# Mixer steps written as two streams between the dense matmuls of a hybrid decoder block

## The chip, the cores and the metric

One core of a Trainium2 chip runs the whole kernel. TensorE (PE) multiplies, VectorE (DVE) and ScalarE (ACT) do elementwise work, GpSimd (POOL) a little, and SyncE (SP) and ACT issue the DMAs. The metric is the device time of one execution in microseconds (us). The kernel before takes 2914.36 us, the median of 3 runs (2911.06 to 2918.03).

## The reference, cut to what matters

One layer over 2048 positions of width 1024, in float32:

```python
h = rmsnorm(x, norm1_g) * (1 + sc1) + sh1
p = h @ w_in                                  # 27 column blocks of 128
ya = rglru_mixer(...)                         # gated linear recurrence, 2 blocks of 128 columns
yb = hgrn2_mixer(...)                         # 6 heads of 64, chunks of 64 positions
yc = rwkv7_mixer(...)                         # 6 heads of 64, delta rule: S = S*w - (S k) (k a)' + v k'
y = concatenate([ya, yb, yc]) * mix_beta
x = x + g1 * (y @ w_out)
h = rmsnorm(x, norm2_g) * (1 + sc2) + sh2
x = x + g2 * ((silu(h @ w_gate) * (h @ w_up)) @ w_down)   # inner width 2816
return rmsnorm(x, final_g)
```

The rows of `p` of one time block must be there before a mixer of that block starts, and all mixers of a block before its product with `w_out`. The state of each mixer goes from one time block to the next.

## The kernel before, in words

The 2048 positions are four time blocks of 512. Activations stand with the 128 columns of a column block on the partitions and 512 positions along the free axis, so a dense product is a row of 128x512 matmuls. Each factor is split into a rounded high part and a low part (`wh`, `wl`; `hh`, `hl`), and each product is three matmuls, `hh*wh`, `hl*wh`, `hh*wl`, written in `project` (line 247). There are 9696 of these **dense matmuls**: 2592 for `w_in`, and 1776 in each block for `w_out`, gate, up and down. ACT rounds a weight tile (`wh`), DVE takes the rest (`wl`, line 220). Four blocks of `w_in` are done first, their results stored in DRAM (`pd`), then `w_out` and the feed-forward part block by block, with the mixers' results (`yd`) read back by `load_y`.

At the end of `w_out` of each block stands the **norm boundary**: the last column's residual (`stt`, DVE), its square, the sum over columns on PE (`rstd_of`, lines 295 to 298), the root (ACT), the scaled input of the feed-forward part (`make_h`, DVE and ACT), and only then the next dense matmul.

The **mixers** are small fp32 matmuls between elementwise steps. For a block, `mixers(b)` writes: the low-rank part `lora`; `rwkv` for head pairs 0 and 1 together; `hgrn` 0; `rglru` 0; `rwkv` for pair 2; `hgrn` 1; `rglru` 1; `hgrn` 2. In `rwkv`, `rwkv_chunks` prepares the chunk operands: after a sum over heads (`blocksum`, lines 256 and 257) come some ten DVE operations of 128x512 and then the matmuls of line 564. Next the small triangular matrices are stored to DRAM (`nd`), and `invert` loads them into `big` by DMAs on ACT's queue (lines 612 and 613; 4 for two pairs, 8 for one), eliminates on DVE, stores the result (`xd`), loads it into `GIQ` and joins halves on PE (lines 643 and 651). Then eight chunks follow each other, each in three steps of PE with DVE and ACT between them (lines 679/681, 692, 697/699). `rglru` loads its rows, convolves on DVE and multiplies (lines 867 and 871). Tiles of `rwkv` have the tag `tr` (9 buffers) and the PSUM tag `pm`, those of the other two `th` (8 buffers) and `ph` (one bank).

The order on each engine is made by the framework's scheduler: it walks through the program by its own estimate of when operands and buffers are ready, and gives each engine, of the instructions that are ready, the one with the lowest priority number. `level(name)` sets these numbers: "out" first, then "load" (weights), "feed" (inputs and norms), "mix", and "dense" last. Within a level the number follows the order of writing. So before, a mixer's matmul goes ahead of any dense matmul as soon as the scheduler holds it for ready, and on DVE and ACT `rwkv` has the right of way over the `hgrn` and `rglru` that are written after it. Once built, each engine runs its list strictly in this order: a matmul that is not ready holds all behind it.

Of the kernel before, what the change touches and what calls it, by code (L numbers as in the profile page):

```python
# [49 lines left out]

@with_exitstack
def hybrid_kernel(ctx, tc, x, par, ada_w, w_in, rgw, igw, w_up, a_up, g_up, w_out,
                  w_gate, w_upf, w_down, cst, msk, out):
    nc = tc.nc
    V, A, G, PE, SP = nc.vector, nc.scalar, nc.gpsimd, nc.tensor, nc.sync
# [193 lines left out]

    def blocksum(src, p, tag):  # L250
        n = src.shape[1]
        hi = tile_of(tag, R)[:, 0:n]
        lo = tile_of(tag, R)[:, 0:n]
        p = p[:, 0:n]
# [217 lines left out]
    def low_rank(i, cols, l1):  # L472
        pz = pm_()
        PE.matmul(pz, LW[i][:, cols], l1, start=True, stop=False)
        PE.matmul(pz, LW[2 + i][:, cols], l1, start=False, stop=True)
        return pz

    def lora(b):

        t = shifted(b, 9, tr_())  # L480
# [36 lines left out]
    def rwkv_chunks(b, u, pr, ld, nd):  # L517

        k = shifted(b, 3 + pr, tr_())
# [12 lines left out]
        rn = rsqrt_of(sq, blocksum(sq, pm_(), "tr"), 1.0, eps_k)  # L532
# [27 lines left out]
        for q in range(0, NCH, 2):  # L560
            ps = pm_()
# [8 lines left out]
        for q in range(0, NCH, 4):  # L570
            p = pm_()
            for c in range(q, q + 4):
                PE.transpose(p[:, (c - q) * 128:(c - q + 1) * 128], BK[:, c, :], ident)
# [8 lines left out]
    def rwkv_values(b, u, pr, r, VS):  # L582

        v = shifted(b, 6 + pr, tr_())
        pb, _ = blocksum(r, pm_(), "tr")
        p = pm_()
        for g in range(NG):
            PE.transpose(p[:, g * 128:(g + 1) * 128], v[:, g * 128:(g + 1) * 128], ident)
# [12 lines left out]
    def invert(b, prs, nd):  # L601
# [8 lines left out]
        for g in range(ng):  # L610
            part = slice(nb * g, nb * g + nb)
            A.dma_start(NL[part], nd)
            A.dma_start(NX[part, 0:32 // ng], n4[:, :, g, :])
        for j in range(1, 31):
# [17 lines left out]
        X1, TT = tr_(), tr_()  # L632
        n = nu * NCH * 32
        xv, tv = (a[:, 0:n].rearrange("p (u c t) -> p u c t", u=nu, t=32) for a in (X1, TT))
        half = [(slice(64 * e, 64 * e + 32), slice(64 * e + 32, 64 * e + 64)) for e in range(2)]
        p = pm_()
        pv = p.rearrange("p (u c t) -> p u c t", u=2, t=32)
        for e, (lo, up) in enumerate(half):
            for u in range(nu):
                V.transpose(X1[lo, u * 256:u * 256 + 256], GIQ[lo, :, u, 0, e, 0:32])  # L640
            for u in range(nu):
                for c in range(NCH):
                    PE.matmul(pv[up, u, c], GIQ[lo, c, u, 0, e, 32:64], xv[lo, u, c], start=True, stop=True)
        for e, (lo, up) in enumerate(half):
            V.tensor_copy(TT[up, 0:n], p[up, 0:n])
        p = pm_()
        pv = p.rearrange("p (u c t) -> p u c t", u=2, t=32)
        for e, (lo, up) in enumerate(half):
            for u in range(nu):
                for c in range(NCH):  # L650
                    PE.matmul(pv[lo, u, c], tv[up, u, c], GIQ[up, c, u, 0, e, 32:64], start=True, stop=True)
# [4 lines left out]
    def rwkv(b, prs, ld):  # L656
# [3 lines left out]
        ops = [rwkv_chunks(b, u, pr, ld, nd) for u, pr in enumerate(prs)]  # L660
        invert(b, prs, nd)
        VS = big_().rearrange("p (c u e v) -> p c u e v", u=2, e=2, v=64)
        bonus = [rwkv_values(b, u, pr, op[3], VS) for u, (pr, op) in enumerate(zip(prs, ops))]
# [9 lines left out]
        for q in range(0, NCH, cq):  # L673
            py = pm_().rearrange("p (c u e t) -> p c u e t", c=cq, u=nu, t=64)
            for c in range(q, q + cq):
                pcn = pp.tile([128, 2, 3, 64], F, name="pc", bufs=1)
                both = [VS[:, c, u].rearrange("p e v -> p (e v)") for u in range(nu)]
                for u, (KG, BK, we, r) in enumerate(ops):
                    PE.matmul(pcn[:, u, 0:2, :], KG[:, c, 0].rearrange("p e t -> p (e t)"), both[u], start=True, stop=True)  # L679
                for u, (KG, BK, we, r) in enumerate(ops):  # L680
                    PE.matmul(py[:, c - q, u], both[u], KG[:, c, 1], start=(c == q and u == 0), stop=False,
# [5 lines left out]
                for u, (KG, BK, we, r) in enumerate(ops):  # L687
                    for e in range(2):
                        s, o = HD[e]
                        act(hw[s, u], VS[s, c, u, e, :], AF.Copy, scale=we[s, c:c + 1])  # L690
                for u in range(nu):
                    PE.matmul(pcn[:, u, 2, :], GIQ[:, c, u, 0].rearrange("p e t -> p (e t)"), rs[:, u], start=True,
                              stop=True)
                V.tensor_copy(VS[0:64, c, 0:nu, 0, :], pcn[0:64, 0:nu, 2, :])
                act(VS[64:128, c, 0:nu, 1, :], pcn[64:128, 0:nu, 2, :])
                for u, (KG, BK, we, r) in enumerate(ops):
                    i1 = PE.matmul(pcn[:, u, 0:2, :], BK[:, c, :], both[u], start=True, stop=True)  # L697
                for u in range(nu):
                    order(PE.matmul(py[:, c - q, u], both[u], GIQ[:, c, u, 1], start=False, stop=True,
# [10 lines left out]
        for y, bn, pr in zip(ys, bonus, prs):  # L710
# [3 lines left out]
            rn = rsqrt_of(sq, blocksum(sq, pm_(), "tr"), 1.0 / 64, eps_g)  # L714
# [4 lines left out]
            A.dma_start(l2, ld[3, 0, :, 0:TB])  # L719
            pg = pm_()  # L720
            PE.matmul(pg, gup[:, cols], l2, start=True, stop=True)
# [10 lines left out]
    def hgrn(b, pr):  # L732
        p = load_p(th_(), 7 + pr, b)
# [12 lines left out]
        pb, _ = blocksum(qk, ph_(), "th")  # L746
# [3 lines left out]
        VS, AQ = big_().rearrange("p (two e c v) -> two p e c v", two=2, e=2, v=64)  # L750
        p = ph_()
        for g in range(NG):
            PE.transpose(p[:, g * 128:(g + 1) * 128], v[:, g * 128:(g + 1) * 128], ident)
# [7 lines left out]
        for l in range(6):  # L761
# [6 lines left out]
            if l == 0:  # L768

                V.tensor_mul(pair, qv[:, :, 1, 0], kv[:, :, 0, 0])  # L770
                pb, _ = blocksum(pair, ph_(), "th")
# [3 lines left out]
            elif l < 4:  # L775

                for e in range(2):
                    s, o = HD[e]
                    z = QZ[s, :, e, :].rearrange("p c (n w) -> p c n w", w=w)
                    act(z, qv[s, :, 1, :].rearrange("p (c n) w -> p c n w", c=NCH))  # L780
                p = ph_()
                for c in range(NCH):
                    PE.matmul(p[0:64, c * 64:c * 64 + 64], k[:, c * 64:c * 64 + 64], QZ[:, c].rearrange("p e t -> p (e t)"),
# [9 lines left out]
            else:  # L793
                p = (ph_(),) * 2
                for c in range(NCH):
                    for j in range(0, 64, 2 * w):
                        for e in range(2):
                            s, o = HD[e]
                            PE.matmul(p[e][o.start + j:o.start + j + w, c * w:c * w + w],
# [15 lines left out]
        KT = c64(th_())  # L815
        p = ph_()
        for g in range(NG):
            PE.transpose(p[:, g * 128:(g + 1) * 128], k[:, g * 128:(g + 1) * 128], ident)
# [5 lines left out]
        for e in range(2):  # L824
            s, o = HD[e]
            p = ph_()
            for c in range(NCH):
                PE.matmul(p[s, c * 64:c * 64 + 64], KT[o, c, :], VS[o, e, c, :], start=True, stop=True)  # L828
            V.tensor_copy(VS[s, e, 0, :], Sc[s, pr, :])
            for c in range(NCH):  # L830
                dst = VS[s, e, c + 1, :] if c + 1 < NCH else Sc[s, pr, :]
                stt(dst, VS[s, e, c, :], dv[s, c:c + 1], p[s, c * 64:c * 64 + 64], OP.mult, OP.add)
        po = ph_()
        for e in range(2):
            s, o = HD[e]
            for c in range(NCH):
                PE.matmul(po[s, c * 64:c * 64 + 64], VS[:, e, c, :], AQ[:, e, c, :], start=True, stop=True)  # L837
# [3 lines left out]
        rn = rsqrt_of(sq, blocksum(sq, ph_(), "th"), 1.0 / 64, eps_n)  # L841
        V.tensor_mul(od, od, rn)
        p = load_p(th_(), 13 + pr, b)
# [12 lines left out]
    def rglru(b, j):  # L856
        up = tile_of("th")
# [6 lines left out]
        for i in range(1, 4):  # L864
            stt(u, up[:, i:i + TB], pc("conv_w", 2 * i + j), u, OP.mult, OP.add)
        p = ph_()
        PE.matmul(p, rgt[:, j, :], u, start=True, stop=True)
        r = th_()
        act(r, p, AF.Sigmoid, bias=pc("rg_b", j))
        p = ph_()  # L870
        PE.matmul(p, igt[:, j, :], u, start=True, stop=True)
# [26 lines left out]
        rn = rsqrt_of(sq, blocksum(sq, ph_(), "th"), 1.0 / 64, eps_n)  # L898
# [4 lines left out]
    def w_in_products(h, cols, side):  # L903

        n = 0
        while n < len(cols):
# [3 lines left out]
            for i, b in enumerate(h):  # L910
                for j, (c, p) in enumerate(zip(cs_, project(h[b], *ws))):
                    with level("feed"):
# [5 lines left out]
                        SP.dma_start(pd[c, :, b * TB:(b + 1) * TB], t)  # L918
                    next(side, None)
            n += len(cs_)  # L920

    def mixers(b):
        with level("mix"):
            lr = lora(b)
            rwkv(b, (0, 1), lr)
            hgrn(b, 0)
            rglru(b, 0)
            rwkv(b, (2,), lr)
            hgrn(b, 1)
            rglru(b, 1)  # L930
            hgrn(b, 2)

    def load_y(b):
        ys = []
# [83 lines left out]
    mixers(0)  # L1018
# [64 lines left out]
```

## Time and profile before

| | |
|---|---|
| median of 3 runs | 2914.36 us |
| the profiled execution | 2919.62 us |
| its span, first to last instruction | 2917.8 us |
| PE busy, weight loads busy | 2767.1 us (95%), 2213.5 us (76%) |
| DVE busy, ACT busy | 1945.5 us (67%), 1480.5 us (51%) |
| mean granted TensorE clock | 0.975 of 2.4 GHz |

Matmuls overlap in the record: a dense one is listed with 399 ns while the next starts 227 ns later. Idle time of PE is what is left of the span: 150.7 us. In the waits view a row tells who waited for whom, the total time, how often, and the longest. The windows view gives for a stretch its length, then for PE, weight loads, DVE, ACT and POOL the busy time and the count of instructions, then the granted clock, the share of DMA and GB/s.

### The profile page before, as it was taken

The page shows a single profiled execution, that of the slowest core. Times are in us where ns is not written, and L with a number is a line of the kernel's source. Part 1 is how long each engine was busy: PE and PEld are TensorE (multiplying, and loading weights), DVE is VectorE, ACT ScalarE, POOL GpSimd, SP SyncE. Part 2 cuts the span into 40 slices and gives each one's busy share as a digit, 9 for nine tenths or more (in the row PEclk, how much of TensorE's full clock was granted, in tenths as well). Part 3 has the DMA queues.
Part 4 walks back from the last instruction along what each step waited for, and adds up shares of the span by engine and source line. Part 5 has one row for each costly group of instructions (what it writes and reads, how often), then busy time and mean ns, then how long its engine had stood idle before and what let it go on. Part 6 is the DMA issues. An engine that isn't in the chain of part 4 may idle for free. (4 is left out here: it accounts for less than half of the span.)

```text
span 2917.8 us, 41296 instructions
## 1 busy us (share of the span) xinstructions
PE 2767.1 (95%) x14842; PEld 2213.5 (76%) x14842; DVE 1945.5 (67%) x4112; ACT 1480.5 (51%) x2472; POOL 86.1 (3%) x67
## 2 busy tenths in 40 slices
PE   7999999999998999999989999998799999999998
PEld 6777777777776777887767778776577888788886
DVE  7676577676757877777787687768776444744345
ACT  5434753564375467536754765377456423533233
POOL 2000000000001000000100000010000001000000
PEclk9999998999998999999989999999899999999999
DMA  7643455454235234341442434233423333433332
GB/s 252 190 138 102 137 182 172 131 159 130 80 124 168 76 103 127 114 107 57 139 145 74 140 111 121 80 113 111 131 77 102 98 98 114 150 98 96 96 98 87
DMA packets 242589, 352.27 MB, mean 121 GB/s; under 512 B 72912, under 2 KB 78544, under 8 KB 242384
## 3 DMA queue, kind: packets, MB, share of 16 engines
q1 hardware_dynamic: 160144, 285.55, 31.6%
q10 hardware_dynamic: 82240, 64.09, 8.3%
q8 instruction: 117, 1.92, 0.3%
q14 instruction: 88, 0.72, 0.1%
HBM read 293.92 MB, written 55.62 MB: 120 GB/s over the span
## 5 line engine op out<-in xcount | busy, mean ns | idle before, releaser
L247 PE MATMUL pd<-hh,wh 128*128 128x512 f32 x3232 | 1288.4, 399 | 33.5 <-ACT hh L78 27.1
L247 PE MATMUL pd<-hl,wh 128*128 128x512 f32 x3232 | 1289.7, 399 | 2.7 <-DVE hl L81 1.4
L247 PE MATMUL pd<-hh,wl 128*128 128x512 f32 x3232 | 1288.2, 399 | 1.1 <-DVE wl L220 1.0
L78 ACT ACTIVATE wh<-wr 128x512 fp32r<-128x512 f32 (+1 forms) x752 | 463.6, 620 | 885.0 <-PE pd L247 707.9
L247 PEld LDWEIGHTS pd<-hh,wh 128*128 128x128 f32 x3232 | 615.1, 191 | 170.0 <-ACT hh L78 32.4
L220 DVE TENSOR_TENSOR wl<-wr,wh 128x512 fp32r<-128x512 f32 (+1 forms) x752 | 511.6, 684 | 321.3 <-ACT wh L78 314.3
L247 PEld LDWEIGHTS pd<-hl,wh 128*128 128x128 f32 x3232 | 614.9, 190 | 137.2 <-DVE hl L81 6.3
L247 PEld LDWEIGHTS pd<-hh,wl 128*128 128x128 f32 x3232 | 615.3, 190 | 131.5 <-issue 5.1
L81 DVE SCALAR_TENSOR_TENSOR xs<-pd,Q,xs 128x512 f32<-128x512 f32 x224 | 167.4, 748 | 152.2 <-PE pd L247 130.4
L78 ACT ACT_TABLE_LOAD x174 | 223.2, 1283 | 3.8 <-PEq L1074 0.7
L78 ACT ACTIVATE th<-th 128x512 f32<-128x512 f32 (+2 forms) x153 | 93.4, 611 | 56.3 <-DVE th L81 14.0
L967 DVE TENSOR_TENSOR xs<-pd,xs 128x512 f32<-128x512 f32 x88 | 60.7, 689 | 83.0 <-PE pd L247 82.7
L78 ACT ACTIVATE xs<-pd 128x512 f32<-128x512 f32 x140 | 82.5, 589 | 45.0 <-PE pd L247 41.5
L78 ACT ACTIVATE hh<-xs 128x512 fp32r<-128x512 f32 x120 | 74.1, 628 | 43.0 <-DVE xs L967 29.1
L78 ACT ACTIVATE hw<-big,we 64x64 f32<-64x64 f32 x192 | 66.2, 345 | 52.1 <-DVE big L81 45.9
L78 ACT ACTIVATE xs<-xs 128x512 f32<-128x512 f32 x77 | 47.8, 627 | 67.9 <-DVE xs L81 38.5
L78 ACT ACTIVATE tr<-tr 128x512 fp32r<-128x512 f32 (+4 forms) x112 | 69.5, 627 | 10.6 <-DVE tr L81 4.7
L539 POOL MEMSET KG<- 64x1024 f32 x24 | 22.7, 946 | 1701.0 <-PE pc L679 839.0
L216 POOL TENSOR_TENSOR hl<-xs,hh 128x512 fp32r<-128x512 f32 x32 | 49.0, 1555 | 642.6 <-ACT hh L78 601.0
L220 DVE TENSOR_TENSOR hl<-xs,hh 128x512 fp32r<-128x512 f32 x88 | 60.7, 690 | 5.6 <-ACT hh L78 1.3
L81 DVE SCALAR_TENSOR_TENSOR big<-pc,we,hw 64x64 f32<-64x64 f32 x168 | 47.6, 283 | 24.7 <-PE pc L697 21.6
L564 PE MATMUL pm<-KG,BK 128*128 128x256 f32 x192 | 50.5, 409 | 11.7 <-DVE KG L553 8.1
(229 smaller groups left out, 2638.7 us busy)
## 6 DMA issues: line engine op xcount, KB each, us to landing
wr<-in_w_gate SPq DMA_DIRECT2D x176, 256.0 KB, 2.6
wr<-in_w_upf SPq DMA_DIRECT2D x176, 256.0 KB, 2.6
wr<-in_w_down SPq DMA_DIRECT2D x160, 256.0 KB, 2.7
wr<-in_w_in SPq DMA_DIRECT2D x144, 256.0 KB, 3.4
pd<-xs SPq DMA_DIRECT2D x108, 256.0 KB, 3.3
xs<-in_x SPq DMA_DIRECT2D x72, 256.0 KB, 4.6
wr<-in_ada_w SPq DMA_DIRECT2D x64, 256.0 KB, 3.4
th<-pd ACTq DMA_DIRECT2D x64, 256.0 KB, 3.8
```

Of the source, the lines that this page charges most:

```text
L78: return A.activation(o, i, f, **k)
L81: return V.scalar_tensor_tensor(o, a, s, b, op0=op0, op1=op1)
L216: G.tensor_sub(lo, src, hi.bitcast(F))
L220: V.tensor_sub(lo, src, hi.bitcast(F))
L247: PE.matmul(p, a[:, c], b, start=(n == 0), stop=(n == tot - 1))
L539: G.memset(KG[o, :, :, e], 0.0)
L564: PE.matmul(ps[:, (c - q) * 256:(c - q + 1) * 256], BK[:, c, :], KG[:, c], start=True, stop=True)
L967: V.tensor_mul(t, pu, t)
```

## The change

Each mixer becomes a generator that yields between its steps, and two streams run through all four blocks: one with `lora` and `rwkv`, one with `hgrn` and `rglru`. After each group of three dense matmuls `tick` moves a clock of the writing on (`now`), and a stream whose time has come writes its next step there. The next time is reckoned from the work that the step put on DVE and ACT, which wrappers around the two engines count (`Counted`).

```diff
+class Counted:                                   # wraps nc.vector, nc.scalar
+                us = self.fixed + int(np.prod(a[0].shape[1:])) / self.rate
+            self.us += us
+            self.free = max(self.free, self.now[0]) + us
...
+    V, A = Counted(nc.vector, 0.16, 960.0), Counted(nc.scalar, 0.2, 1200.0)
...
                         PE.matmul(p, a[:, c], b, start=(n == 0), stop=(n == tot - 1))
+                    now[0] += 0.68
+                tick()
...
+    def step(s):
+        v, a, d = V.us, A.us, A.dmas
+        with level("mix"):
+            extra = next(s["steps"], None)
+        v, a, d = V.us - v, A.us - a, A.dmas - d
+        s["at"] = max(now[0] + max(v, a) + 0.5 * min(v, a) + (2.0 if d else 0.0), V.free, A.free) + (extra or 0.5)
+    def mm(*a, **k):
+        with level("dense"):
+            now[0] += 0.15
+            return PE.matmul(*a, **k)
...
     def blocksum(src, p, tag):
         split_v(src, hi, lo)
-        PE.matmul(p, bones, hi, start=True, stop=False)
-        return p, PE.matmul(p, bones, lo, start=False, stop=True)
+        yield
+        p = bank_()[:, 0:n]
+        mm(p, bones, lo, start=True, stop=False)
+        return p, mm(p, bones, hi, start=False, stop=True)
...
         for q in range(0, NCH, 2):
+            yield
             ps = pm_()
             for c in range(q, q + 2):
-                PE.matmul(ps[:, (c - q) * 256:(c - q + 1) * 256], BK[:, c, :], KG[:, c], start=True, stop=True)
+                mm(ps[:, (c - q) * 256:(c - q + 1) * 256], BK[:, c, :], KG[:, c], start=True, stop=True)
...
+    def mixers_a(s):
+        for b in range(NB):
+            ld = yield from lora(b)
+            yield from rwkv(b, (0, 1), ld)
+            yield from rwkv(b, (2,), ld)
+            s["block"] = b + 1
+    def mixers_b(s):
+        for b in range(NB):
+            while streams[0]["block"] < b:
+                yield 1.0
+            yield from hgrn(b, 0)
+            yield from rglru(b, 0)
+            yield from hgrn(b, 1)
+            yield from rglru(b, 1)
+            yield from hgrn(b, 2)
+            s["block"] = b + 1
...
     def load_y(b):
+        finish(b)
...
-        if b + 1 < NB:
-            mixers(b + 1)
```

All matmuls and transposes of the mixers are now written through `mm` and `transpose`, at the level "dense", so that among matmuls that are ready the order of writing decides; their DVE and ACT work stays at "mix". `needs` holds a step back until its rows of `p` are written, `finish(b)` writes what is left of block `b` before its results are loaded. The scheduler still has the last word: a mixer matmul that it does not hold for ready where it was written goes in later. The program has as many instructions on each engine as before, but for one activation table load less (232 for 233).

What this does to the order is shown at two places. The first is the norm boundary of the second time block on PE, the last dense matmuls of `w_out` and the first of the feed-forward part. Before (256/257 are a `blocksum` of `hgrn`, 296 to 298 the norm's sum, 753 a transpose of `hgrn`):

```order
L247 MATMUL pd<-hl,wh 128x512
L247 MATMUL pd<-hh,wl 128x512
L256 MATMUL ph<-th,bones 128x512
L257 MATMUL ph<-th,bones 128x512
L296 MATMUL pd<-wh,aones 128x512
L297 MATMUL pd<-wl,aones 128x512
L298 MATMUL pd<-xs,aones 128x512
L753 MATMUL ph<-C,th 128x128 x4
L247 MATMUL pd<-hh,wh 128x512 x2
```

and now (365 to 367 are the norm's sum, 304 stands in `mm`, here the matmuls of `invert`):

```order
L273 MATMUL pd<-hh,wl 128x512
L365 MATMUL pd<-wh,aones 128x512
L273 MATMUL pd<-hh,wh 128x512
L273 MATMUL pd<-hl,wh 128x512
L366 MATMUL pd<-wl,aones 128x512
L273 MATMUL pd<-hh,wl 128x512
L367 MATMUL pd<-xs,aones 128x512
L304 MATMUL pm<-tr,GIQ 32x32 x24
L273 MATMUL pd<-hh,wh 128x512 x2
```

The `blocksum` is gone from the place ahead of the norm's sum, and 24 matmuls of `invert` stand between that sum and the next dense matmul.

The second place is ACT's queue at the same boundary. Before, just ahead of the norm (`xs<-xs` are the squares of the last columns, the DMAs are the loads of `invert` for pair 2 of the third block):

```order
L612 DMA big<-nd_2_13094 32x1024
L613 DMA big<-nd_2_13094 32x8x32
L612 DMA big<-nd_2_13094 32x1024
L78 ACTIVATE xs<-xs 128x512
L613 DMA big<-nd_2_13094 32x8x32
L612 DMA big<-nd_2_13094 32x1024
L613 DMA big<-nd_2_13094 32x8x32
L78 ACTIVATE xs<-xs 128x512
L612 DMA big<-nd_2_13094 32x1024
L613 DMA big<-nd_2_13094 32x8x32
```

and now (line 71 is the helper that passes an ACT instruction on):

```order
L71 ACTIVATE xs<-xs 128x512
L71 DMA GIQ<-xd_0_12266 32x8x32 x2
L71 ACTIVATE wh<-xs 128x512
L71 ACTIVATE wh<-wr 128x512 x3
L71 ACT_TABLE_LOAD
L71 DMA GIQ<-xd_0_12266 32x8x32 x2
L71 ACTIVATE wh<-wr 128x512
L71 ACTIVATE rstd<-pd,epsc 128x512
L71 DMA GIQ<-xd_0_12266 32x8x32
L71 ACT_TABLE_LOAD
L71 ACTIVATE rstd<-rstd 128x512
L71 DMA GIQ<-xd_0_12266 32x8x32 x2
```

The eight loads of `big` stood among the squares; now eight loads of `GIQ` (for pairs 0 and 1 of the third block) stand among the steps of the root. In the program of before, eight loads of `big` stand ahead of the norm in the same way at the boundaries of the first and the third block too. Now there are none at the first, and at the third the four loads of pairs 0 and 1 of the last block.

## Rows read from the trace of the kernel before

**Rows 1.** The page, busy time, share and count of each engine.

```profile
PE 2767.1 (95%) x14842; PEld 2213.5 (76%) x14842; DVE 1945.5 (67%) x4112; ACT 1480.5 (51%) x2472; POOL 86.1 (3%) x67
```

**Rows 2.** Span and mean granted clock of the core.

```profile
core 0: 2917.8 us, clock 0.975
```

**Rows 3.** Windows of 100 us, one with mixers, one without.

```profile
1500.00:1600.00 100.00, 86.64 (x565) 66.69 (x566) 77.03 (x206) 50.71 (x102) 0.00 (x0) 0.91 0.28 83
...
2600.00:2700.00 100.00, 100.00 (x442) 82.79 (x442) 42.89 (x64) 29.00 (x47) 0.00 (x0) 1.00 0.33 98
```

**Rows 4.** Whom PE waited for, whole span: us in total, times, longest.

```profile
PE pd L247 <- ACT hh L78: 27.1, 8, 4.5
PE ph L256 <- ACT th L78: 14.7, 8, 6.1
...
PE ph L867 <- DVE th L81: 12.9, 4, 6.6
PE pm L564 <- DVE KG L553: 8.1, 5, 5.4
PE pm L643 <- DVE tr L640: 8.0, 6, 3.4
...
PE pm L256 <- ACT tr L78: 6.3, 6, 3.8
```

**Rows 5.** Timeline of PE, boundary of the second block: start, us, in brackets idle before.

```profile
1506.06 0.80 PE L256 MATMUL ph<-th,bones 128*128 128x512 f32 x1 [6.09 <-ACT th L78]
...
1510.97 2.07 PE L298 MATMUL pd<-xs,aones 128*128 128x512 f32 x2 [2.27 <-DVE xs L280]
...
1517.61 1.22 PE L247 MATMUL pd<-hh,wh 128*128 128x512 f32 x2 [3.72 <-ACT hh L78]
```

**Rows 6.** Timeline of ACT and its DMA queue just before it.

```profile
1496.30 0.63 ACT L78 ACTIVATE xs<-xs 128x512 f32<-128x512 f32 x1 [5.66 <-DMA out<-xs]
1496.32 0.60 ACTq L613 DMA_DIRECT2D big<-nd  x1
...
1502.68 0.63 ACT L78 ACTIVATE xs<-xs 128x512 f32<-128x512 f32 x1 [5.75 <-DVE xs L81]
```

**Rows 7.** Whom PE waited for, 2040 to 2085 us, boundary of the third block.

```profile
PE pd L247 <- DVE xs L81: 5.0, 1, 5.0
PE pd L247 <- ACT hh L78: 4.3, 1, 4.3
PE pd L296 <- ACT wh L78: 2.8, 1, 2.8
PE pd L298 <- DVE xs L280: 2.6, 1, 2.6
```

**Rows 8.** The same, 940 to 970 us, boundary of the first block.

```profile
PE pd L247 <- ACT hh L78: 4.5, 1, 4.5
```

**Rows 9.** Timeline of PE, last block's boundary, no mixers left.

```profile
2535.63 1.12 PE L298 MATMUL pd<-xs,aones 128*128 128x512 f32 x2 [1.57 <-DVE xs L280]
...
2541.01 1.22 PE L247 MATMUL pd<-hh,wh 128*128 128x512 f32 x2 [4.26 <-ACT hh L78]
```

**Rows 10.** Windows of 20 us at three boundaries; the clock follows POOL's count.

```profile
1500.00:1520.00 20.00, 7.92 (x15) 3.92 (x16) 15.75 (x36) 12.89 (x21) 0.00 (x0) 0.62 0.38 122
...
2060.00:2080.00 20.00, 10.06 (x35) 6.38 (x34) 17.82 (x56) 11.23 (x19) 0.00 (x0) 0.79 0.28 86
...
2540.00:2560.00 20.00, 18.97 (x73) 15.04 (x74) 14.81 (x23) 11.05 (x17) 0.00 (x0) 0.85 0.18 54
```

**Rows 11.** Timeline of PE, from a head sum to the convolution's matmul.

```profile
1940.66 0.79 PE L257 MATMUL ph<-th,bones 128*128 128x512 f32 x1
...
1978.20 1.22 PE L867 MATMUL ph<-th,rgt 128*128 128x512 f32 x1 [6.56 <-DVE th L81]
```

**Rows 12.** Timeline of PE, from a head sum to the chunk operands' matmuls.

```profile
673.10 0.40 PE L257 MATMUL pm<-tr,bones 128*128 128x512 f32 x1
...
703.40 1.19 PE L564 MATMUL pm<-KG,BK 128*128 128x256 f32 x2 [5.36 <-DVE KG L553]
```

More of the change, by code (lines that the diff above doesn't have):

```diff
@@ L247, in project, with tick, finish, transpose @@
                         PE.matmul(p, a[:, c], b, start=(n == 0), stop=(n == tot - 1))
-        return ps
+                    now[0] += 0.68
+                tick()
+        return ps
+    now, streams = [0.0], []
+    V.now = A.now = now
+    def tick():
+        for s in streams:
+            while s["block"] < NB and now[0] >= s["at"]:
+                step(s)
+    def step(s):
[4 more added lines that the diff above has]
+        s["at"] = max(now[0] + max(v, a) + 0.5 * min(v, a) + (2.0 if d else 0.0), V.free, A.free) + (extra or 0.5)
+    def finish(b):
+        for s in streams:
+            while s["block"] <= b:
+                step(s)
+    def mm(*a, **k):
+        with level("dense"):
+            now[0] += 0.15
+            return PE.matmul(*a, **k)
+    def transpose(*a):
+        with level("dense"):
+            now[0] += 0.15
+            return PE.transpose(*a)
+    def needs(b, *cols):
+        while not all((c, b) in stored for c in cols):
+            yield 1.0
+    stored = set()
     def blocksum(src, p, tag):
         n = src.shape[1]
+        bank_ = p
         hi = tile_of(tag, R)[:, 0:n]
         lo = tile_of(tag, R)[:, 0:n]
-        p = p[:, 0:n]
         split_v(src, hi, lo)
-        PE.matmul(p, bones, hi, start=True, stop=False)
-        return p, PE.matmul(p, bones, lo, start=False, stop=True)
+        yield
+        p = bank_()[:, 0:n]
+        mm(p, bones, lo, start=True, stop=False)
+        return p, mm(p, bones, hi, start=False, stop=True)
     def rsqrt_of(r, p, scale, eps, table=None):
@@ L473, in low_rank @@
         pz = pm_()
-        PE.matmul(pz, LW[i][:, cols], l1, start=True, stop=False)
-        PE.matmul(pz, LW[2 + i][:, cols], l1, start=False, stop=True)
+        mm(pz, LW[i][:, cols], l1, start=True, stop=False)
+        mm(pz, LW[2 + i][:, cols], l1, start=False, stop=True)
         return pz
     def lora(b):
+        yield from needs(b, 25, 26)
         t = shifted(b, 9, tr_())
@@ L517, in rwkv_chunks @@
     def rwkv_chunks(b, u, pr, ld, nd):
+        yield from needs(b, 16 + pr, 19 + pr)
         k = shifted(b, 3 + pr, tr_())
@@ L531, in rwkv_chunks @@
         act(sq, k, AF.Square, scale=pc("k_k", pr))
-        rn = rsqrt_of(sq, blocksum(sq, pm_(), "tr"), 1.0, eps_k)
+        rn = rsqrt_of(sq, (yield from blocksum(sq, pm_, "tr")), 1.0, eps_k)
         kap = tr_()
@@ L640, in invert @@
                 V.transpose(X1[lo, u * 256:u * 256 + 256], GIQ[lo, :, u, 0, e, 0:32])
[L641 to L645, printed above, removed]
+        yield
         p = pm_()
@@ L650, in invert @@
                 for c in range(NCH):
-                    PE.matmul(pv[lo, u, c], tv[up, u, c], GIQ[up, c, u, 0, e, 32:64], start=True, stop=True)
+                    mm(pv[up, u, c], GIQ[lo, c, u, 0, e, 32:64], xv[lo, u, c], start=True, stop=True)
+        for e, (lo, up) in enumerate(half):
+            V.tensor_copy(TT[up, 0:n], p[up, 0:n])
+        yield
+        p = pm_()
+        pv = p.rearrange("p (u c t) -> p u c t", u=2, t=32)
+        for e, (lo, up) in enumerate(half):
+            for u in range(nu):
+                for c in range(NCH):
+                    mm(pv[lo, u, c], tv[up, u, c], GIQ[up, c, u, 0, e, 32:64], start=True, stop=True)
         for e, (lo, up) in enumerate(half):
@@ L732, in hgrn @@
     def hgrn(b, pr):
+        yield from needs(b, 4 + pr, 7 + pr, 10 + pr)
         p = load_p(th_(), 7 + pr, b)
@@ L745, in hgrn @@
         v = load_p(th_(), 10 + pr, b)
-        pb, _ = blocksum(qk, ph_(), "th")
+        pb, _ = yield from blocksum(qk, ph_, "th")
         od = qk
@@ L770, in hgrn @@
                 V.tensor_mul(pair, qv[:, :, 1, 0], kv[:, :, 0, 0])
-                pb, _ = blocksum(pair, ph_(), "th")
+                pb, _ = yield from blocksum(pair, ph_, "th")
                 vv, ov = (a.rearrange("p (n two) -> p n two", two=2) for a in (v, od))
@@ L840, in hgrn @@
         act(sq, od, AF.Square)
-        rn = rsqrt_of(sq, blocksum(sq, ph_(), "th"), 1.0 / 64, eps_n)
+        rn = rsqrt_of(sq, (yield from blocksum(sq, ph_, "th")), 1.0 / 64, eps_n)
         V.tensor_mul(od, od, rn)
+        yield from needs(b, 13 + pr)
         p = load_p(th_(), 13 + pr, b)
@@ L856, in rglru @@
     def rglru(b, j):
+        yield from needs(b, j, 2 + j)
         up = tile_of("th")
@@ L918, in w_in_products @@
                         SP.dma_start(pd[c, :, b * TB:(b + 1) * TB], t)
+                        stored.add((c, b))
                     next(side, None)
             n += len(cs_)
[L922 to L931, printed above, removed]
+    def mixers_a(s):
[7 more added lines that the diff above has]
+            while streams[0]["block"] < b:
+                yield 1.0
+            yield from hgrn(b, 0)
[4 more added lines that the diff above has]
+            s["block"] = b + 1
+    for f in (mixers_a, mixers_b):
+        s = {"block": 0, "at": 0.0}
+        s["steps"] = f(s)
+        streams.append(s)
     def load_y(b):
+        finish(b)
         ys = []
```

87 lines of the change are left out of this document (60 added, 27 removed).

## The prediction

> **What bounds the kernel now.** I read the page's busy shares first: PE is busy 95% of the span, DVE 67%, ACT 51% [rows 1]. Then the windows: where no mixer is left, PE is busy all the time and starts 442 matmuls in 100 us, one per 0.226 us [rows 3]. The 9696 dense matmuls at that pace are 2191 us; the rest of the 2917.8 us [rows 2] is the mixers' own matmuls, which the change neither adds to nor takes from, and PE's waits with the slow clock behind them. So PE is the bound, and the change can move only waits: 2917.8 - 2767.1 = 150.7 us of idle time, and the clock that was not granted, (1 - 0.975) x 2917.8 = 73 us of full speed, a part of which falls into the idle time itself. Third, the waits of PE: they are of two kinds. Dense matmuls wait for ACT's `hh` after a norm, 27.1 us in 8 waits. Mixer matmuls wait for DVE and ACT, and everything behind them waits too: 14.7, 12.9, 8.1, 8.0 and 6.3 us in the five largest groups, together 50.0 [rows 4].
>
> **The norm boundaries.** In the last block, with no mixers left, the boundary costs 4.26 + 1.57 = 5.8 us of waiting [rows 9]. In the first its longest wait is 4.5 [rows 8], so about the same. In the second it is 6.09 + 2.27 + 3.72 = 12.1 [rows 5], in the third 5.0 + 4.3 + 2.8 + 2.6 = 14.7 [rows 7]. What those two have and the others lack is both of two things at once: the stores of the previous block's final norm, which hold the `xs` buffers, and the loads of `big` in ACT's queue. A square waited 5.66 us for such a store, with a load right behind it, and the next waited 5.75 us for the residual [rows 6]. In the first 6.09 a `blocksum` stands at the head of PE's queue, though, and the norm's sum behind it could not have gone earlier either, since its squares came late too.
>
> The excess over the bare boundary is 12.1 - 5.8 = 6.3 and 14.7 - 5.8 = 8.9, together 15.2 us. Now the eight loads of `big` are gone from the second boundary, but eight loads of `GIQ` stand there among the steps of the root, behind a store to DRAM that they must wait for, and 24 matmuls of `invert` stand ahead of the feed-forward's first matmul; at the third, four loads stand for eight. From below: all 15.2 goes, and the 24 matmuls fill some of the bare wait. From above: what waits now is the load of `GIQ`, and each place costs 6 us more than today, as the longest wait of today does [rows 5]. I take half the excess, -7.6 us, since one cause of the two is removed at one place and halved at the other.
>
> **The mixers' waits.** The groups sum to 50.0, of which 6.09 is counted above: 43.9 us. A mixer's matmul waits when DVE or ACT need longer than the dense matmuls placed in between last, so I counted these in both programs.
>
> - Convolution (line 867): 12.9 us. In the worst case PE reached it 37.5 - 6.6 = 30.9 us after the last head sum, and it was ready after 37.5 [rows 11]. Over the eight places the dense matmuls in between are 636 before, 764 now, 20% more; six of eight get more, one falls from 73 to 59, the one with the 6.56 us wait from 133 to 108. Half goes: -6.
> - Head sums of `hgrn` and `rglru` (line 256, `ph`): 14.7 - 6.1 = 8.6 left. Both parts of a sum now stand together, after the low part, so ACT's cast has DVE's operation as additional time. Half goes: -4.
> - Joining of the inverse (643): 8.0 us. For two pairs the distance grows from 171 to 223 dense matmuls to 186 to 441, for one pair it falls from 199 to 276 to 211 to 227. A quarter goes: -2.
> - Chunk operands (564): 8.1 us, and head sums of `rwkv` 6.3 [rows 4]: no change taken; the first is the slower rival below.
>
> Sum -12 us. From below it could be -43.9, all of it; from above +38, by the rival. I take -12, as most matmuls keep the distance that the scheduler's own estimate gives them: counted in the built program, only a quarter of the mixers' matmuls stand where they were written, and the middle one comes 75 dense matmuls later.
>
> **The clock.** In 1500 to 1520 us PE was idle for 12.1 us and was granted 0.62, so (1 - 0.62) x 20 = 7.6 us of full speed were withheld; in 2060 to 2080, 9.9 us idle and 4.2 us withheld [rows 10]. Spread evenly over the stretch, 40% and 50% of that hits busy time: 3.0 and 2.1 us, some 0.2 us per us of idle time. If all of it hits busy time, as the slow clock follows the idle time rather than falling into it, it is 0.4 to 0.6. I take 0.4: (7.6 + 12) x 0.4 = 7.8 us.
>
> The Trainium skill, "TensorE: Matmul & The Clock Gate" (Terms), reckons the penalty as the throttled time times the withheld share, so all of the 7.6 us counts. By it the clock term would be 0.63 x 19.6 = 12.3 us and the sum 4.5 us lower. The trace does not settle it: its windows show the idle time and the clock, not which came first.
>
> **What costs nothing.** The instructions are the same on every engine but one table load. The mixers end later among the dense matmuls, after 7375 of them (before: 6998), but `w_out` of the last block begins only at 7920; 545 x 0.226 = 123 us of cover. If that were gone, `load_y` would wait for the last mixers at its full length. DVE and ACT keep the weights' split ahead of the mixers as before.
>
> **Sum.** -7.6 - 12 - 7.8 = -27.4. The profiled execution took 2919.6 us, 1.8 more than its span, so 2892 by its own time. It lies 5.2 us above the median of the runs, which gives 2887. A measurement here tells 0.2% from no change, 6 us, so this would be seen.
>
> **Rivals.**
>
> *The chunk operands become late: slower.* Between the head sum of `rwkv_chunks` and line 564 stand 57 to 156 dense matmuls before, 1150 over the twelve places, and now 60 to 130, 983 in all. For it: the worst place took 30.3 us with 106 dense matmuls in between and still waited 5.36 us [rows 12]; there now stand 90. And `hgrn`'s work on DVE, which stood behind `rwkv`'s, now has equal right of way. Against it: PE waited for `KG` 5 times, 8.1 us in all [rows 4], so most of the twelve distances had room. If DVE needs as long as before everywhere, PE waits 167 x 0.226 = 38 us more, with the clock 38 x 1.4 = 53: 2887 + 53 = 2940. It decides from a wait of 27.4 / (12 x 1.4) = 1.6 us more at each of the twelve.
>
> *Nothing changes.* The scheduler's estimate sets three quarters of the places in both programs, and where that estimate errs against the chip, it errs in both; other matmuls wait instead. For it: the number of switches from a dense to a mixer matmul is 482 before and 479 now. Against it: the places of collision have moved at two boundaries. Then 2914, within 6 us.
>
> *All these waits go.* If the written distances cover DVE and ACT everywhere, 43.9 + 15.2 = 59.1 us go, with the clock 83: 2919.6 - 83 - 5 = 2832. For it: at a quarter of the places the matmul now has more room than the estimate asked for. Against it: a place with a fifth fewer dense matmuls ahead of it exists in each group.
>
> The Trainium skill, "Perfetto Trace Analysis" (Identifying the Most-Contended Engine), says that matmul busy time does not tell the distance from the bound, the busy time of weight loads does. The row has 76% for these against 95% [rows 1], and 82.8% where PE never waits [rows 3]. By that rule the floor is 2213.5 / 0.828 = 2673 us, so the third rival would have more room than 151 us. The trace agrees only in part: small fp32 matmuls load fewer weights per time than dense ones.
>
> **How the numbers follow.** The forecast 0.52, its own range 2852 to 2903 (the first two terms doubled with the clock at 0.6, or halved with it at 0.2: 39 x 1.6 = 62 and 9.8 x 1.2 = 12 us off 2914); the slower rival 0.22; no change 0.15; all waits gone 0.11. Faster by over 0.2%: nearly all of the first and the last, 0.61; within: 0.16; slower: 0.23. The range for 8 in 10 takes in most of both outer rivals, 2840 to 2936.
>
> **What the profile would show.** Right: the idle time before line 867's matmul under 7 us, the waits at the second and third boundary between 6 and 12 us each, mean granted clock 0.977 or more, PE idle near 131 us. Wrong: waits on `KG` before the matmuls of 564 above 20 us (the slower rival); a wait for `GIQ` or for the transposed tiles at 643 at the second boundary (the bound from above); DVE's share above 85% where mixers run; or dense matmuls that wait for `wl` or `wh`, which they hardly do today.

## The result and the profile after

The changed kernel takes 2867.06 us (median of 4 runs, 2864.06 to 2878.97), the kernel before, beside it on the same chip, 2916.2 us (4 runs): a ratio of 0.984, 95% interval 0.980 to 0.987. The forecast was 2887 with a range of 2840 to 2936: right in sign and range, 20 us too high. The profiled execution took 2866.1 us with a span of 2864.3, against 2892 forecast by its own time.

The page's first part and the core's row, of after:

```profile
PE 2740.4 (96%) x14842; PEld 2193.8 (77%) x14842; DVE 1935.9 (68%) x4112; ACT 1476.2 (52%) x2471; POOL 81.8 (3%) x67
```

```profile
core 0: 2864.3 us, clock 0.983
```

Beside [rows 1, 2] the counts are the same but for one table load on ACT, and the span is 53.5 us shorter. PE's idle time fell from 150.7 to 2864.3 - 2740.4 = 123.9, by 26.8 us; its busy time fell by 26.7. Both halves need an explanation.

Whom PE waited for, over the whole span (us in total, times, longest). Lines 304 and 309 are the helpers through which every mixer's matmul is now written, so one goes by the tiles:

```profile
PE pd L273 <- ACT hh L71: 22.1, 6, 8.2
...
PE pm L304 <- DVE KG L71: 10.2, 9, 5.1
PE pm L304 <- DVE tr L71: 8.4, 8, 2.9
PE ph L304 <- DVE th L71: 7.9, 10, 2.3
PE pc L304 <- ACT rs L71: 6.8, 7, 4.6
PE pd L367 <- DVE xs L71: 5.7, 3, 2.0
PE pd L273 <- ACT xs L71: 3.9, 1, 3.9
PE ph L309 <- DVE th L71: 3.6, 4, 1.8
```

The head sums of `hgrn` and `rglru` and the convolution's matmul no longer lead [rows 4]; the chunk operands (`KG`) stay where they were. The groups by line and shape (count, busy us, mean ns, idle us before them) show the convolution, the joining of the inverse, and the head sums:

```profile
L304 PE MATMUL pm<-tr,bones 128*128 128x512 f32 x72 | 25.1, 429 | 2.5 <-DVE tr L71 2.3
...
L304 PE MATMUL ph<-th,bones 128*128 128x512 f32 x64 | 22.4, 426 | 5.7 <-DVE th L71 4.3 <-DVE big L71 0.7 <-DVE we L71 0.4
L304 PE MATMUL pm<-tr,GIQ 32*32 32x32 f32 x384 | 16.2, 198 | 6.2 <-DVE tr L71 6.2
...
L304 PE MATMUL ph<-th,rgt 128*128 128x512 f32 x16 | 8.6, 618 | 1.7 <-DVE th L71 1.7
```

The timeline of PE at the second block's norm boundary, the place of [rows 5]:

```profile
1442.74 1.13 PE L367 MATMUL pd<-xs,aones 128*128 128x512 f32 x2 [2.04 <-DVE xs L71]
1443.79 0.69 PE L304 MATMUL pm<-tr,GIQ 32*32 32x32 f32 x16
1446.27 1.72 PE L304 MATMUL pm<-tr,GIQ 32*32 32x32 f32 x32 [1.79 <-DVE tr L71]
1448.12 1.22 PE L273 MATMUL pd<-hh,wh 128*128 128x512 f32 x2
1450.01 0.80 PE L273 MATMUL pd<-hl,wh 128*128 128x512 f32 x1 [0.67 <-DVE hl L71]
```

Of 12.1 us 2.04 + 1.79 + 0.67 = 4.5 are left, less than the bare 5.8 of the last block: matmuls of the inverse stand in the gap (16 + 32 in these rows; the trace lists each of the program's 24 twice), and `hh` is there when they end. At the third, the place of [rows 7], 2.04 + 4.54 = 6.6 of 14.7 are left:

```profile
1987.04 1.40 PE L367 MATMUL pd<-xs,aones 128*128 128x512 f32 x2 [2.04 <-DVE xs L71]
1988.37 1.97 PE L304 MATMUL ph<-big,th 64*64 64x64 f32 x16
1994.88 1.22 PE L273 MATMUL pd<-hh,wh 128*128 128x512 f32 x2 [4.54 <-ACT hh L71]
```

At the first boundary, where before the dense matmul waited 4.5 us for `hh` [rows 8], a matmul of `rwkv`'s chunks now waits about as long just ahead of it:

```profile
924.63 1.12 PE L304 MATMUL pc<-rs,GIQ 128*128 128x64 f32 x4 [4.57 <-ACT rs L71]
```

A new wait stands elsewhere, the longest of after but for 13.6 us at the kernel's start, at the first norm of a later block. PE's row, and those of DVE and ACT ahead of it:

```profile
471.57 0.79 PE L273 MATMUL pd<-hh,wh 128*128 128x512 f32 x1 [8.24 <-ACT hh L71]
...
470.01 0.75 DVE L71 SCALAR_TENSOR_TENSOR xs<-xs,Q,rstd 128x512 f32<-128x512 f32 x1 [4.16 <-DMA xs<-in_x]
...
470.79 0.72 ACT L71 ACTIVATE hh<-xs,Q 128x512 fp32r<-128x512 f32 x1 [4.67 <-DVE xs L71]
```

Both engines stood idle there: the load of `x` that they needed was issued at 464.10 us and landed at 469.98.

Windows of 20 us at the second and third boundary (the clock follows POOL's count), for [rows 10]: PE is idle for 4.6 and 6.6 us instead of 12.1 and 9.9.

```profile
1440.00:1460.00 20.00, 15.37 (x88) 11.23 (x88) 16.24 (x26) 13.41 (x18) 0.00 (x0) 0.74 0.34 89
1985.00:2005.00 20.00, 13.41 (x48) 9.71 (x49) 16.91 (x38) 9.93 (x15) 0.00 (x0) 0.66 0.08 28
```

### The profile page after: what moved, and what is told of

The parts are those of the page before. It is cut to its first block, busy times and chain, and to the rows that moved or that the text cites. A ratio compares the mean times of both kernels' runs of the same rounds, so it can differ in the third digit from the quotient of the medians.

```text
span 2864.3 us, 41250 instructions
## 1 busy us (share of the span) xinstructions
PE 2740.4 (96%) x14842; PEld 2193.8 (77%) x14842; DVE 1935.9 (68%) x4112; ACT 1476.2 (52%) x2471; POOL 81.8 (3%) x67
## 4 chain that ended last, share of the span: by engine, by line
PE 76%; DVE 11%; DMA 6%; ACT 4%; issue 3%; POOL 0%; SPq 0%; ACTq 0%; DVEq 0%; POOLq 0%
PE pd L273 62%; PE pm L304 5%; PE ph L304 4%; DVE xs L71 3%; PE pc L304 2%; DVE wl L71 2%; DVE big L71 2%; DVE th L71 1%; DVE tr L71 1%; DMA wr<-in_ada_w 1%; DMA tr<-ld 1%; ACT th L71 1%; ACT wh L71 1%; DMA xs<-in_x 1%; ACT L71 1%
## 5 line engine op out<-in xcount | busy, mean ns | idle before, releaser
L71 DVE TENSOR_TENSOR th<-th 128x256 f32<-128x256 f32 (+8 forms) x349 | 155.6, 463 | 30.1 <-ACT th L71 24.4
L71 DVE TENSOR_TENSOR big<-big 128x30 f32<-128x30 f32 (+7 forms) x480 | 113.0, 235 | 11.9 <-DMA big<-nd 0.9
L71 ACT ACTIVATE hh<-xs 128x512 fp32r<-128x512 f32 x120 | 73.8, 626 | 36.5 <-DVE xs L71 25.3
L71 ACT ACTIVATE tr<-tr 128x512 fp32r<-128x512 f32 (+4 forms) x112 | 69.5, 626 | 18.2 <-DVE tr L71 17.0
```

The lines of the kernel that those rows point to most:

```text
L71: return f(*a, **k)
```

## The experiments

Two theories stood after this. P: a mixer's matmul, written at its place by the estimate, leaves DVE and ACT the time they need. S: two streams with equal right of way fill each other's waits and take the inverse's loads off the boundaries. Times are medians; each ratio is to the kernel before, measured beside it.

| kernel | streams | estimate | us | ratio, 95% interval |
|---|---|---|---|---|
| after | 2 | x1.0 | 2867 | 0.984 (0.980 to 0.987) |
| e1_mix_level | 2 | x1.0 | 2868 | 0.984 (0.982 to 0.985) |
| e14_two_90 | 2 | x0.9 | 2866 | 0.982 (0.980 to 0.983) |
| e10_faster | 2 | x0.8 | 2870 | 0.984 (0.983 to 0.985) |
| e14_two_60 | 2 | x0.6 | 2872 | 0.984 (0.982 to 0.986) |
| e3_no_estimate | 2 | none | 2982 | 1.023 (1.021 to 1.025) |
| e9_slower | 2 | x1.25 | 3310 | 1.135 (1.133 to 1.137) |
| e8_one_free_mix | 1 | none | 2912 | 0.998 (0.997 to 0.999) |
| e13_one_50 | 1 | x0.5 | 2919 | 1.000 (0.999 to 1.001) |
| e13_one_70 | 1 | x0.7 | 2958 | 1.013 (1.012 to 1.015) |
| e2_one_stream | 1 | x1.0 | 3298 | 1.131 (1.130 to 1.133) |
| e4_loads_on_sp | kernel before | | 2922 | 1.002 (1.001 to 1.003) |
| e6_no_loads | kernel before | | 2880 | 0.987 (0.986 to 0.989) |

**The level of the mixers' matmuls.**

```diff
     def mm(*a, **k):
-        with level("dense"):
+        with level("mix"):
...
```

(and the same in `transpose`)

> The changed kernel with one edit: the mixers' matmuls and transposes are given the scheduler's level of the rest of the mixers ("mix", as before the change) instead of that of the dense products. Theory P (what helps is that a mixer's matmul is held at its written place among the dense ones, so that DVE and ACT have time before it): the matmuls run ahead again, most of the gain goes, 2900 us or more, PE idle 140 us or more. Theory S (what helps is that two streams with equal right of way keep the loads of the inverse off the norm boundaries and fill DVE's and ACT's gaps): 2867 us within 10, PE idle 120 to 130 us, the two boundaries still under 8 us of waiting each.

The same time as after, PE idle 124.9 us, the two boundaries 6.7 and 7.1 us. P in this form falls: holding the matmul at its written place is not what helps.

**One stream.**

```diff
-    for f in (mixers_a, mixers_b):
+    for f in (mixers_a,):
```

(with the old order of mixers inside it)

> The changed kernel with one stream of steps instead of two, its mixers in the order from before the change (lora, rwkv of pairs 0 and 1, hgrn 0, rglru 0, rwkv of pair 2, hgrn 1, rglru 1, hgrn 2); steps, estimate and levels stay. Theory P (placing by steps): 2867 to 2885 us, the boundaries and the convolution's matmul as after the change. Theory S (two streams): 2905 us or more, with the waits before the convolution's matmul or at the norm boundaries back (over 8 us and over 20 us for the second and third boundary together).

3298 us: over the 2905 that S named, but through something neither theory had. The mixers no longer fit: a step waits for the estimate of the one ahead, the block's chain is longer than the dense products beside it, and `finish` writes the rest in a lump ahead of `load_y`. A window of 100 us there, and PE's timeline in it:

```profile
1400.00:1500.00 100.00, 36.91 (x270) 26.44 (x269) 58.24 (x127) 57.88 (x82) 4.11 (x3) 0.57 0.24 70
```

```profile
1405.61 1.22 PE L304 MATMUL pm<-tr,LW 128*128 128x512 f32 x2 [5.57 <-ACT tr L71]
...
1429.98 1.22 PE L304 MATMUL ph<-th,bones 128*128 128x512 f32 x2 [17.16 <-DVE th L71]
```

PE is busy 37%, no dense matmul stands in the window's first 43 us, and the wait of a head sum, which dense matmuls cover elsewhere, is bare: 17.2 us.

**No estimate.**

```diff
-        s["at"] = max(now[0] + max(v, a) + 0.5 * min(v, a) + (2.0 if d else 0.0), V.free, A.free) + (extra or 0.5)
+        s["at"] = now[0] + 0.5
```

> The changed kernel without the estimate: the next step of a stream is written 0.5 units of the dense clock after the last one, whatever DVE and ACT have queued. If the estimate does the work: the mixers' matmuls stand too early, 2895 us or more, with waits on KG, on the transposed tiles and on the convolution's input over 50 us together. If the scheduler's own estimate places them anyway: 2867 us within 10 and the waits as after the change.

The estimate is needed: 2982 us. But the waits are not the ones I expected all over the span; about half of the loss stands in one stretch:

```profile
880.00:980.00 100.00, 63.36 (x409) 47.89 (x410) 53.11 (x150) 43.88 (x90) 7.32 (x6) 0.56 0.19 56
```

```profile
888.89 2.14 PE L304 MATMUL pm<-tr,GIQ 32*32 32x32 f32 x32 [12.84 <-DVE tr L71]
891.54 1.73 PE L304 MATMUL pm<-GIQ,tr 32*32 32x32 f32 x32 [0.51 <-DVE tr L71]
895.65 1.22 PE L304 MATMUL pm<-tr,bones 128*128 128x512 f32 x2 [2.38 <-DVE tr L71]
```

In the built program 203 matmuls of the mixers (380 in the trace's rows) stand together there, after the 2628th dense one, with `rwkv`'s and `hgrn`'s mixed; a second row of 106 comes before the third boundary. Without pacing the two streams crowd DVE and ACT, and the first to be needed is not the first to be done. That this is the reason for the 203 is argued from the order, not shown.

**The inverse's loads on another queue**, in the kernel before:

```diff
-            A.dma_start(NL[part], nd)
-            A.dma_start(NX[part, 0:32 // ng], n4[:, :, g, :])
+            SP.dma_start(NL[part], nd)
+            SP.dma_start(NX[part, 0:32 // ng], n4[:, :, g, :])
```

> The kernel before with one edit: the loads of `big` for the inverse (the two of lines 612 and 613) are issued from SP instead of ACT. If the waits at the second and third norm boundary come from ACT standing behind these loads in its queue: 12.1 + 14.7 = 26.8 us of waiting there falls to 16 or less, the time to about 2895 us. If they come from the DMA engines being shared, or the loads are innocent: the waits stay at 22 us or more and the time is 2916 us within 8.

Nothing gained, and the boundaries are worse, 15.6 and 15.9 us. ACT at the second boundary, and PE:

```profile
1492.87 0.64 ACT L78 ACTIVATE xs<-xs 128x512 f32<-128x512 f32 x1 [3.40 <-DMA out<-xs]
1499.01 0.63 ACT L78 ACTIVATE xs<-xs 128x512 f32<-128x512 f32 x1 [5.50 <-DVE xs L81]
1502.56 0.63 ACT L78 ACTIVATE xs<-xs 128x512 f32<-128x512 f32 x1 [2.92 <-DVE xs L81]
1504.14 0.63 ACT L78 ACTIVATE wh<-xs 128x512 fp32r<-128x512 f32 x1 [0.95 <-DVE xs L277]
```

```profile
1504.83 0.79 PE L296 MATMUL pd<-wh,aones 128*128 128x512 f32 x1 [9.10 <-ACT wh L78]
```

The squares wait as in [rows 6]; now the norm's own sum waits 9.1 us for them. So the head sum that stood first in PE's queue before was not the cause. Whether the loads are, this run does not say: SP's queue carries the stores of `out`, which they may hold back.

**The loads left out**, in the kernel before:

```diff
-        for g in range(ng):
-            part = slice(nb * g, nb * g + nb)
-            A.dma_start(NL[part], nd)
-            A.dma_start(NX[part, 0:32 // ng], n4[:, :, g, :])
+        V.memset(t[:, 0:1536], 0.0)
```

> The kernel before with the inverse's loads of `big` left out (a memset in their place, so the inverse is computed of zeros): the loads' collision with the norm boundaries alone. If the loads cause the excess of the second and third boundary, wherever they are queued: both fall to 5.8 to 7 us of waiting (from 12.1 and 14.7), about 15 us of idle time and 10 to 15 us of slow clock go, some 2890 us. If the excess comes from the stores of the final norm or from the blocksum ahead of it alone: the two boundaries keep over 20 us together and the time is 2905 us or more (the inverse itself may still start earlier).

PE at the second and the third boundary:

```profile
1557.29 0.49 PE L296 MATMUL pd<-wh,aones 128*128 128x512 f32 x1 [0.72 <-ACT wh L78]
1558.18 0.50 PE L297 MATMUL pd<-wl,aones 128*128 128x512 f32 x1 [0.40 <-DVE wl L220]
1561.74 2.08 PE L298 MATMUL pd<-xs,aones 128*128 128x512 f32 x2 [3.05 <-DVE xs L280]
1568.07 1.22 PE L247 MATMUL pd<-hh,wh 128*128 128x512 f32 x2 [4.26 <-ACT hh L78]
```

```profile
2083.52 1.13 PE L298 MATMUL pd<-xs,aones 128*128 128x512 f32 x2 [1.57 <-DVE xs L280]
2088.91 1.22 PE L247 MATMUL pd<-hh,wh 128*128 128x512 f32 x2 [4.26 <-ACT hh L78]
```

The third is the bare boundary of [rows 9] to the hundredth; the second, 8.4 us in these rows, keeps 2.6 of its excess of 6.3. The stores of `out` differ too: at the second four of them were issued 15.5 to 4.2 us ahead of the next dense matmul (before, the last six 25.3 to 19.6), at the third the last landed 24.1 us ahead of it (before, 18.2). So without the loads most of the excess goes, which bears the prediction's collision out; whether the loads cost by their place in ACT's queue or by their traffic beside the stores stays open. The kernel after agrees: at its second boundary the last five stores were issued 27.7 to 18.6 us ahead, about as before, no load of `big` stands near, and neither ACT nor DVE waits for a store. The 38 us gained are more than the boundaries: the inverse starts earlier and the mixers behind it move, so they are no price of the loads alone.

**One stream without an estimate**, which leaves the finer steps and `blocksum`'s order: e2's and e3's edits together, with e1's.

> The changed kernel with one stream in the order from before, no estimate, and the mixers' level for their matmuls: what is left of the change is the finer steps, blocksum's order and the places where banks are taken. If the gain comes only from streams and estimate together: 2914 us within 10, as before the change. If the finer steps bring it: 2885 us or less.

2912 us: the steps alone bring 0.2%.

**Longer and shorter estimates.** The kernel after with both engines' durations times 1.25, 0.8, 0.9 and 0.6, here 0.8:

```diff
-    V, A = Counted(nc.vector, 0.16, 960.0), Counted(nc.scalar, 0.2, 1200.0)
+    V, A = Counted(nc.vector, 0.128, 1200.0), Counted(nc.scalar, 0.16, 1500.0)
```

> The changed kernel with the estimate's durations on DVE and ACT 1.25 times as long. If a step written later only gets more room: 2855 to 2870 us. If the streams have just enough time until the next block needs them: what is left is written in a lump ahead of `load_y` (up to 281 matmuls of the mixers stand together in the built program), PE waits there as with one stream, 3200 us or more with a granted clock under 0.92.

> The changed kernel with the estimate's durations on DVE and ACT 0.8 times as long. If the estimate is what gives each matmul its room: waits on DVE and ACT before the mixers' matmuls grow, 2880 to 2895 us. If any pacing does that keeps the two streams in step and the scheduler places the matmul by readiness: 2867 us within 8, with other single waits in place of the present ones.

> The changed kernel with 0.9 times the estimate's durations. Between 1.0 (2867 us) and 0.8 (2870 us): 2868 us within 6 if nothing hangs on the estimate's value while the streams keep in step; a single late matmul may move it by 5 us either way.

> The changed kernel with 0.6 times the estimate's durations. If the room given to each matmul counts: 2890 us or more, a good way towards the 2982 us without an estimate. If only the two streams' balance counts: 2870 us within 8.

From 0.6 to 1.0 nothing changes that these runs can separate well, with other single waits each time (`hh` 9.2 us in all at 0.9, 42.2 at 0.8). So the room that the estimate gives a matmul where it is written is not the gain: P falls in its second form too. At 1.25 the lumps come, as said: 3310 us, clock 0.899.

**One stream with an estimate that fits.** e2 with 0.7 and 0.5 times the durations:

> The one-stream kernel with the estimate's durations on DVE and ACT 0.7 times as long, so that its steps are spread over the dense products and end just before the next block needs them (the longest row of the mixers' matmuls together is 35 in the built program, but for 94 at the very end). If pacing that fits the block is what counts: 2860 to 2880 us. If two streams with equal right of way are needed: 2905 us or more.

> The same with 0.5 times the durations. In the built program the matmuls end after 7059 dense ones (before the change: 6998), so it should be near the time of before: 2895 to 2915 us by either theory; under 2880 us, if any pacing is enough.

2958 and 2919 us. At 0.7 some lumps are left, the largest at the last block:

```profile
2480.00:2530.00 50.00, 19.62 (x182) 14.23 (x183) 19.64 (x43) 19.20 (x30) 5.49 (x4) 0.57 0.12 37
```

so that run is no clean test; at 0.5 there is none, and the time is that of before. One stream was no better than 2912 us at any of four paces, two were 2866 to 2872 at four paces. The gain takes both: the second stream, and a pace that keeps the two together and ends in time. Either alone loses or gives 0.2% at most. Not tried were a pace between 0.5 and 0.7 for one stream, and one under 0.6 for two.

How the two streams do it is not one thing. What the five versions with two streams paced at 0.6 to 1.0 (e1 among them) share is the total: PE is idle for 124 to 132 us, against 150.7 before and 152.1 and 162.6 with one stream (no estimate, 0.5). The split differs: at 0.9 the mixers' matmuls wait 76.4 us over the whole span, more than the 72.3 of before, and the dense ones 20.4 for 37.3; at 0.8 it is 46.7 and 49.1, and the second and third boundary take 9.7 and 9.1 us, though no load of `big` was issued in the 60 us ahead of either. So S holds as to the streams; that keeping the loads off the boundaries is what they gain by is not shown.

No version beat the changed kernel measurably; 0.9 times the estimate (0.982, within its interval) has its speed and stands further from the cliff.

## Why the prediction was right, and what it mis-sized

The mechanism was right: PE is the bound, the same instructions run, waits go and the clock follows. The 53.5 us less of span, beside the terms of the sum:

- *Norm boundaries: -7.6 forecast, -15.7 measured* (26.8 to 4.5 + 6.6 = 11.1 in the rows above). I took half the excess of 15.2; all of it went, as the bound from below had it. The step that failed is "one cause of the two is removed at one place and halved at the other". At the second boundary the stores, about where they had been, held up nothing once the loads were gone. At the third the four loads stand in the queue, but were issued 49 to 42 us ahead of the next dense matmul (before, the eight 37 to 25 us), the stores 58 to 28 us ahead (38 to 24), so the collision was not halved there but gone. My bound from above did show, a wait for the transposed tiles at the joining of the inverse, with 1.8 us instead of 6, and it stands in time that `hh` would have taken anyway. That sign of "wrong" was badly chosen: it told of filling.
- *Mixers' waits: -12 forecast, -16 measured* (PE's idle time before all mixers' matmuls off the four boundaries, 65.6 to 49.5 us). By group: convolution 12.9 to 1.7 (forecast -6); joining 8.0 to 4.4, beside the 1.8 at the second boundary (-2); `KG` from 8.1 + 3.0 to 10.2 (no change); head sums of `hgrn` and `rglru` from 8.6 for the high part and 3.5 for the low to 5.7 for both (-4); of `rwkv` from 6.5 to 2.5 (none was forecast). Rows of before that are not shown above:

```profile
L564 PE MATMUL pm<-KG,BK 128*128 128x256 f32 x192 | 50.5, 409 | 11.7 <-DVE KG L553 8.1 <-DVE KG L568 3.0 <-DVE BK L549 0.3
...
L257 PE MATMUL ph<-th,bones 128*128 128x512 f32 x32 | 14.6, 458 | 3.5 <-DVE th L220 3.4
...
L867 PE MATMUL ph<-th,rgt 128*128 128x512 f32 x16 | 11.1, 779 | 12.9 <-DVE th L81 12.9
```

  These five groups fell by 25 us, twice the 12; all other matmuls of the mixers, which my term held at nothing, wait 9 us more, as `ph<-C,th` (0.3 to 3.7) and `pm<-tr,gup` (0 to 3.2). Counting the dense matmuls in between gave the right direction for the convolution and the joining; that the sum came within 4 us is luck in part, and at 0.9 times the estimate these waits did not fall at all (67 us).
- *Waits of dense matmuls elsewhere: nothing forecast, +6 measured* (off the four boundaries 15.5 to 21.8 us), the 8.24 us at 471.6 us ahead of them, where a load of `x` landed late. The rest of the idle time, the first boundary and other norms among it, fell by 1.3.
- *The clock: -7.8 forecast; PE's busy time fell by 26.7.* This is the term that was mis-sized most. Withheld were 73 us of full speed before; now it is (1 - 0.983) x 2864.3 = 49. Summed over the clock's records where PE runs matmuls it is 49.3 before and 34.0 after: -15.3, or 0.57 us per us of idle time gone, where I took 0.4 for 19.6 us only. The step that failed is the price read from the windows of [rows 10], spread between the evenly spread loss and the full one: the clock is low in stretches, 17 before and 11 after, and a wait that vanishes can take its stretch with it. The price is no constant: reckoned alike, e1 and the paces 0.9, 0.8 and 0.6 give 0.8, 0.9, 1.0 and 0.8 us. The other 11.4 us of busy time I can't place; matmuls right behind a wait show longer durations (the convolution's mean 618 ns now, 779 before), which may be part of it. It is hardly chance, as 8 to 9 us recur in each of those four versions. Its cause stays open.

The sum: -15.7 - 16 + 6.2 - 1.3 - 15.3 - 11.4 = -53.5, against -27.4.

Of the signs of "right", the convolution's 1.7 us, the third boundary's 6.6 and the clock's 0.983 came as said; the second boundary (4.5 us) and PE's idle time (123.9) fell below what I gave. Of those of "wrong", beside the joining's, one came in part: DVE is busy for 86.7 of the 100 us from 1900 us on, though for under 82 in every other such window.

The Trainium skill, "TensorE: Matmul & The Clock Gate" (Terms), counts all of the throttled time times the withheld share. With the measured clock that is 73 - 49 = 24 us, near the 26.7 of PE's busy time; only 15.3 of it lies beside matmuls by the records, so that nearness may be chance. As a price per us of idle time its 0.63 came nearer to the 0.57 measured than my 0.4, so the trace rather speaks for the rule.

The rivals: the chunk operands did not become late; `KG` cost 10.2 us in 9 waits, not 38 more. One of 5.06 us is left at 1890 us, like the 5.36 of [rows 12]. "Nothing changes" rested on the scheduler placing most matmuls whatever is written. That is half true: at e1's edit and at any pace from 0.6 to 1.0 the time stays. It does not hold for the streams, which decide what is ready. Of *all these waits go*, 15.7 + 25 of its 59.1 us went, but others came in their place.

The prediction's picture, the distance in built order against DVE's time, is not refuted by e1 and the paces, which change where a matmul is written. Over the eight places between the last head sum and the convolution stood 636 dense matmuls before and 764 after; in the other four versions with two paced streams 901 to 1074, with 0.3 to 2.0 us of waiting in all; with one stream 664 (no estimate) and 643 (0.5), with 12.6 and 15.0 us. But at 555 (one stream, 0.7), 571 (e3) and 650 (e6) the wait was only 0.4, 4.0 and 2.2 us, so distance alone does not decide. And the prediction missed the danger: that the estimate, a quarter longer, leaves the mixers in a lump ahead of `load_y`. I had priced their later end at nothing by 123 us of cover at the last block, which held, but the cover goes all at once.

## What to carry to other kernels

When one engine is the bound and its waits come from a chain of small steps on others, try two independent chains beside each other before you tune the distance within one; pace them so that they stay together. Test the pace from both sides: here it is flat from 0.6 to 1.0 and costs 15% at 1.25, so leave a margin to the side where work is left over. Price a wait on the bound engine by its idle time and by the slow stretch it brings, as the difference of two profiles and not as an average over one. And judge such a change by PE's idle time as a whole: single waits come and go from version to version, while the total stays.

## What the runs showed of the hardware

The granted clock fell to half, the lower of its two levels, in 17 stretches before and 11 after, most of them beside waits of 2 to 8 us; where PE was busy 37% of 100 us its mean was 0.57. The two halves of the gain, idle and busy time, were as large as each other (26.8 and 26.7 us), which I had not expected of a change that only moves waits. And moving the inverse's loads from one engine's DMA queue to another's did not free the boundary: its waits went from 26.8 to 31.5 us.
